# Program order in place of scheduling: the context and Fourier stage of a hybrid mixer block, and the ends of its output rows

## The chip, the cores and the metric

The kernel runs on one core of a Trainium2 chip. The metric is the device time of one launch in microseconds, lower is better. The core has TensorE (PE in the profile, with its weight loads as PEld), VectorE (DVE), ScalarE (ACT), GpSimd (POOL) and SyncE (SP, whose queue issues most DMAs). Each works through its own queue in order; semaphores tie the queues together.

## The reference

One layer of a diffusion backbone on 1024 latent tokens of 1024 channels, and 256 context tokens that are only read. A normalised input is projected once; three branches (neighbourhood attention, Fourier mixing, a convolution module) are gated, projected, merged and projected out.

```python
h  = rms_norm(x, g_pre) * (1 + scale) + shift
hc = rms_norm(ctx, g_pre) * (1 + scale_c) + shift_c
kc, vc = split(hc @ w_in[:, 512:1536])
q, k, v, g_a, u_f, g_f, c_a, c_b, g_c, s_a, s_f, s_c = split(h @ w_in)
attn = neighbourhood_attention(q, k, v, kc, vc, rpb)    # 8 x 16 window, and all context keys
f = real(fftn(u_f in 4 groups of 64, axes=(position, channel), norm="ortho"))
u = c_a * sigmoid(c_b)
u = depthwise_conv(u, w_dw, width=31) + b_dw            # 256 channels
u = silu(layer_norm(u, ln_g, ln_b)) @ w_pw              # channel norm, pointwise map
y_a, y_f, y_c = (attn * silu(g_a)) @ p_attn, ((f @ w_four) * silu(g_f)) @ p_four, (u * silu(g_c)) @ p_conv
merged = sigmoid(s_a) * y_a + sigmoid(s_f) * y_f + sigmoid(s_c) * y_c
return x + gate * rms_norm(merged @ w_out, g_post)
```

## The kernel before

Everything is float32. A product of two float32 matrices is done as three matmuls on a high and a low part of each operand (`mm3`, L141 to L143): high with high, and each high with the other's low. To split an operand, ScalarE casts it to the high part (`whi`, `hi`) and POOL or DVE subtracts (`wlo`, `lo`), both at L93. Weights come from HBM as `raw`, are split and then used; few are held, so the split of a weight waits until an earlier one is no longer read.

The stages follow each other: normalised input and the convolution's input projection (to 72 us), the context and Fourier stage with values, keys of the context and the convolution's taps (to about 226), the channel norm and the pointwise map woven into the attention's first key and query products (to 275), attention (to 480), gates, products of weight blocks in pairs, the branch projections (to 845) and the output product.

In the context and Fourier stage TensorE's work is a generator, `main_b`, whose steps are 6 or 12 matmuls; `adv(n)` takes n steps. After each step it adds `tap["rate"]` to a counter and calls `taps` for each whole one. A tap is one DVE instruction of the depthwise convolution (L476): an accumulator gets the shifted input `u` times a column. `cacc` holds the two channel blocks' results, `cb_` the odd taps. The fold (`e`, `o`, L721) turns the Fourier input into even and odd parts, which are split; `wch`, `wcl` are products of small transform matrices, split again; `eo` are the products with the long transform matrices, which arrive as weights.

TensorE alone is in program order there (`manual_schedule(engines={PE})`). For the other four the scheduler of the framework chooses the order, within program order for the chain of taps and with the first tap held behind the scaling of the context tokens (`after(..., ctx_scaled[-1])`). The channel norm comes after the stage, in pools and PSUM banks of its own: pairs of channel blocks are added and split, a matmul with ones gives `mean`, squares give `pv_`, POOL raises it to -0.5 (`rs`), a diagonal `dg` and a matmul spread it (`rsb`), and DVE and ScalarE make the swish input `zz`, 512 tokens (a half, h = 0 or 1) and one channel block at a time.

In the tail all five engines follow program order. `project(d)` makes the d-th block of 128 merged channels; `mg` is that block, and each half of it is a sum of three gated products, two additions per half (L1636). `side(d, h)` puts other work between. The output product is done in four blocks n = NP to NP + 3, each for two rows of 128 tokens, as seven products p1 to p7 of combined operands (`c0`, `c1`, ..., from `a11`, `a12` and sums `w`) with weights `wo`; `x`, `y` and `z` are PSUM banks, and `s1`, `u2`, `u3`, `s5` are copies of a bank taken between products (L1301, L1303). g2, g3, g7 add copies into quarter results; `flush` runs the end of finished quarters: square, scale, add to the rows `xt` that `x_load` fetched, store.

Of the kernel before, what the change touches and what calls it, by code (L numbers as in the profile page):

```python
# [11 lines left out]
F32 = mybir.dt.float32  # L12
# [40 lines left out]
def block_kernel(ctx: ExitStack, tc: tile.TileContext, x, ctxt, wmodp, wgate,  # L53
# [391 lines left out]
    u = [cv.tile([P, UW], F32, name=f"u{c}") for c in range(2)]  # L445
# [24 lines left out]
    cb_ = cv.tile([P, 512], F32, name="cb_")  # L470

    def fir(acc, src, ws, n, first=None):
        for k, w in enumerate(ws):
            v = src[:, k:k + n]
            if k > 0:
                tc.keep_in_program_order(dve.scalar_tensor_tensor(  # L476
                    out=acc, in0=v, scalar=w, in1=acc, op0=ALU.mult, op1=ALU.add))
            elif first is None:
                after(dve.tensor_scalar(out=acc, in0=v, scalar1=w, scalar2=None, op0=ALU.mult), ctx_scaled[-1])
# [21 lines left out]
    ca1 = [cv.tile([P, 512], F32, name=f"ca1{h}") for h in range(2)]  # L501
# [17 lines left out]
    man.enter_context(tc.manual_schedule(engines={mybir.EngineType.PE}))  # L519
    fx = ExitStack()  # L520
# [159 lines left out]

    cxs = ExitStack()
# [3 lines left out]
    ctx_scaled = [f() for f in [norm_scale(t, cx, cz, "junk") for t in cts]]  # L685
    adv(12)
# [29 lines left out]
    def fold(c):  # L716
# [8 lines left out]
        eh, el = bp.tile([P, 512], F32R, name=f"eh{c}"), bp.tile([P, 512], F32R, name=f"el{c}")  # L725
        oh, ol = bp.tile([P, 512], F32R, name=f"oh{c}"), bp.tile([P, 512], F32R, name=f"ol{c}")
# [31 lines left out]

    ae = []
# [13 lines left out]
    edge = []  # L773
    for m in range(2):
# [99 lines left out]
    psw = pools(lx, name="psw", bufs=2, space=PSUM)  # L874
    psc = pools(lx, name="psc", bufs=1, space=PSUM)
    main = main_l()
    tap["rate"] = 0.0
    adv(6)
    pwh, pwl = half_load(w_pw.rearrange("(k p) c -> p k c", p=P), [P, 2, 256], "pw", bp, b2, "lnq")
    omat = bp.tile([P, P], F32R, name="omat")  # L880
    act.activation(omat, ones, AF.Copy, scale=1.0 / 256.0)
    yc = [bp.tile([P, T], F32, name=f"yc{m}") for m in range(2)]
    vs8 = bp.tile([P, 8], F32, name="vs8")
    halves = [slice(h * 514, h * 514 + 512) for h in range(2)]

    def split_ln(src):
        hi = b2.tile([P, 512], F32R, tag="lnh", name="hi", bufs=4)
        lo = b2.tile([P, 512], F32R, tag="lnl", name="lo", bufs=4)
        split(src, hi, lo, dve)
        return hi, lo  # L890

    def pair_sum(v0, v1):
        t = b2.tile([P, 512], F32, tag="lnt", name="t")
        dve.tensor_tensor(out=t, in0=v0, in1=v1, op=ALU.add)
        return split_ln(t)

    cs = [pair_sum(cacc[0][:, s], cacc[1][:, s]) for s in halves]
    sqs = []
    for h, s in enumerate(halves):
        adv((1, 1)[h])  # L900
        mean = psw.tile([P, 512], F32, tag="sw", name="mean")
        for i in range(2):
# [988 lines left out]
```

## Time and profile before

| | |
|---|---|
| median of 3 runs | 942.32 us (941.96 to 943.43) |
| the profiled execution's own time | 943.67 us |
| its span | 941.9 us |
| TensorE busy | 890.4 us, 95% |
| VectorE busy | 725.9 us, 77% |
| ScalarE and GpSimd busy | 413.8 and 341.9 us |
| DMA | 135.85 MB |
| TensorE's granted clock, mean | 0.985 |

The span goes from the first to the last instruction; the rest of an execution's time lies around it. A row of a timeline has the start, the duration, the engine, the line and operation, the output and inputs by the program's names, the shape, and in brackets how long the engine had been idle and what it waited for. A row of a stretch has its limits, its length, then the busy time of each engine, the granted clock of TensorE, the busy share of DMA and the GB/s moved.

### The profile page before, as it was taken

What the parts mean: (1) busy time and instruction counts of PE and PEld (TensorE: products, weight loads), DVE (VectorE), ACT (ScalarE), POOL (GpSimd) and SP (SyncE); (2) the same over time, 40 slices, a digit from 0 to 9 for tenths busy, and PEclk for the clock granted to TensorE, in tenths of its full rate; (3) what the DMA queues carried; (4) which work ended last, traced back from release to release, by engine and by line L of the source; (5) the groups of instructions that cost most, each with busy time, mean ns of one, the idle gap of its engine ahead of it and who ended that gap; (6) DMA issues with size and microseconds to landing.
All of it is one profiled execution on the core that took longest, in us unless ns stands there. A gap on an engine that the chain in (4) does not pass through costs nothing. (4 is left out here: it accounts for less than half of the span.)

```text
span 941.9 us, 13235 instructions
## 1 busy us (share of the span) xinstructions
PE 890.4 (95%) x4652; PEld 746.4 (79%) x4652; DVE 725.9 (77%) x1183; ACT 413.8 (44%) x830; POOL 341.9 (36%) x310
## 2 busy tenths in 40 slices
PE   4899989999899999999999989999999999998896
PEld 2578889988678888888888877788878888775685
DVE  4656897596768999999959786557864679997985
ACT  4344523233456766776643444333343521225441
POOL 2123822164234434444420003335652048570232
PEclk9999989999999999999999999999999999999999
DMA  9703024345434444544323236423313799851323
GB/s 366 277 13 122 23 78 147 112 140 181 119 104 146 135 145 128 162 128 134 124 79 114 72 130 230 126 80 109 112 58 88 245 349 328 288 204 40 109 90 134
DMA packets 114162, 135.85 MB, mean 144 GB/s; under 512 B 5680, under 2 KB 83760, under 8 KB 114096
## 3 DMA queue, kind: packets, MB, share of 16 engines
q1 hardware_dynamic: 113952, 134.43, 43.5%
q0 software_dynamic: 144, 0.59, 0.3%
q8 instruction: 36, 0.59, 0.3%
q14 instruction: 30, 0.25, 0.1%
HBM read 102.03 MB, written 29.36 MB: 139 GB/s over the span
## 5 line engine op out<-in xcount | busy, mean ns | idle before, releaser
L141 PE MATMUL ps<-hh,whi 128*128 128x512 f32 x304 | 126.7, 417 | 0.9 <-DVE qd L851 0.9
L93 POOL TENSOR_TENSOR wlo<-raw,whi 128x512 fp32r<-128x512 f32 (+2 forms) x52 | 79.1, 1539 | 119.5 <-ACT whi L93 107.3
L143 PE MATMUL ps<-hh,wlo 128*128 128x512 f32 x304 | 119.6, 394 | 0.0
L142 PE MATMUL ps<-hl,whi 128*128 128x512 f32 x304 | 119.6, 393 | 0.0
L93 DVE TENSOR_TENSOR c<-w,c 128x512 fp32r<-128x512 f32 x64 | 53.0, 865 | 30.0 <-ACT c L93 29.9
L93 ACT CAST whi<-raw 128x512 fp32r<-128x512 f32 (+2 forms) x65 | 43.8, 705 | 69.7 <-PE ps L142 27.9
L1636 POOL TENSOR_TENSOR mg<-mg,th 128x512 f32<-128x512 f32 x30 | 50.6, 1687 | 62.3 <-DVE th L1633 60.7
L1013 POOL TENSOR_TENSOR bias<-mk,braw 128x288 f32<-128x288 bf16 (+1 forms) x64 | 54.2, 848 | 38.8 <-DVE mn L1045 37.6
L143 PEld LDWEIGHTS ps<-hh,wlo 128*128 128x128 f32 x304 | 57.5, 189 | 12.7
L141 PEld LDWEIGHTS ps<-hh,whi 128*128 128x128 f32 x304 | 57.7, 190 | 11.1 <-PE ps L143 1.3
L142 PEld LDWEIGHTS ps<-hl,whi 128*128 128x128 f32 x304 | 57.8, 190 | 9.7 <-issue 0.5
L1078 ACT CAST pt<-tp 96x384 fp32r<-96x384 f32 (+1 forms) x96 | 46.1, 514 | 43.0 <-PE tp L1071 42.3
L1084 DVE TENSOR_TENSOR pt<-tp,pt 96x384 fp32r<-96x384 f32 (+1 forms) x96 | 54.4, 593 | 2.9 <-ACT pt L1078 1.4
L1045 DVE CUSTOM_DVE_ANT_0 pr<-scb,bias 128x544 f32<-128x544 f32 (+1 forms) x64 | 49.4, 772 | 8.5 <-PE scb L1038 7.7
L1266 POOL TENSOR_TENSOR w<-raw 128x512 f32<-128x512 f32 x9 | 13.8, 1538 | 109.6 <-DMA raw<-in_w_in_dram 99.6
L1052 ACT ACTIVATE pr<-pr,mn 128x544 f32<-128x544 f32 (+1 forms) x64 | 50.8, 794 | 3.7 <-DVE mn L1045 3.6
L143 PE MATMUL ps<-gh,wlo 128*128 128x512 f32 x128 | 50.0, 390 | 0.7 <-DVE wlo L93 0.7
L141 PE MATMUL ps<-gh,whi 128*128 128x512 f32 x128 | 50.3, 393 | 0.0
L142 PE MATMUL ps<-gl,whi 128*128 128x512 f32 x128 | 50.0, 390 | 0.2 <-DVE gl L93 0.2
L1071 PE MATMUL tp<-ident,pr 128*128 128x128 f32 (+1 forms) x320 | 45.8, 274 | 1.4 <-DVE rc L1058 1.0
L93 ACT CAST c<-w 128x512 fp32r<-128x512 f32 x64 | 37.1, 617 | 22.7 <-DVE w L1266 19.5
L141 PE MATMUL x<-t,c 128*128 128x512 f32 x96 | 39.1, 407 | 6.5 <-ACT s L1301 3.3
(498 smaller groups left out, 2639.3 us busy)
## 6 DMA issues: line engine op xcount, KB each, us to landing
raw<-in_w_in_dram SPq DMA_DIRECT2D x51, 512.0 KB
wt<-in_wmodp_dram SPq DMA_DIRECT2D x16, 512.0 KB
thd<-th SPq DMA_DIRECT2D x32, 256.0 KB
th<-thd SPq DMA_DIRECT2D x32, 256.0 KB
braw<-in_rpbp_dram SPq DMA_DIRECT2D x32, 192.0 KB
vt<-vd SPq DMA_DIRECT2D x48, 128.0 KB
vd<-vs SPq DMA_DIRECT2D x20, 256.0 KB
vt<-vd SPq DMA_DIRECT2D x48, 96.0 KB
```

The source lines that it names most:

```text
L93: return act.copy(hi, src), (lo_eng or pool).tensor_tensor(out=lo, in0=src, in1=f32(hi), op=ALU.subtract)
L141: pe.matmul(ps, wh, mh, start=start, stop=False, **kw)
L142: pe.matmul(ps, wh, ml, start=False, stop=False, **kw)
L143: pe.matmul(ps, wl, mh, start=False, stop=stop, **kw)
L1013: pool.tensor_tensor(out=dst, in0=mk[:, a * 3 + MJ[j], 0:n].rearrange("p (r w) -> p r w", w=W), in1=raws[h_, min(j, 1)][:, :, 0:W], op=ALU ...
L1045: dve.tensor_tensor_reduce(out=pr, in0=sc, in1=biases[h_][:, FULL[h_](n)], scale=1.0, scalar=BIG, op0=ALU.add, op1=ALU.min, accum_out=mn)
L1052: act.activation(pr, pr, AF.Exp, scale=-1.0, bias=mn, accum_out=sums)
L1071: pe.transpose(tp[0:(kw if b < 3 else P), b], src, ident)
L1078: act.copy(pt[0:q, b0:b1, 0], tp[0:q, b0:b1])
L1084: dve.tensor_tensor(out=pt[0:q, b0:b1, 1], in0=tp[0:q, b0:b1], in1=f32(pt[0:q, b0:b1, 0]), op=ALU.subtract)
L1266: (pool if 2 < n < NP else dve).tensor_tensor(out=t, in0=i0, in1=i1, op=op)
L1636: eng.tensor_tensor(out=mg[d][:, s], in0=mg[d][:, s], in1=t, op=ALU.add)
```

## The change

Two parts, in two places of the program.

In the context and Fourier stage a second manual schedule, `bman`, covers all five engines from the stage's start to the end of the channel norm, so each engine's queue is in program order. The holds on the taps are gone. Taps are dealt by `tap["rate"]`, which is set at eight places, with taps by hand before and after the context's scaling; after the last, one step of TensorE's work goes with each tap until the taps are used up. The channel norm and the pointwise map become a generator, `channel_norm`, that says after each piece how many steps of TensorE's work come next, and it runs inside the stage, on tiles of the stage that are free by then (`oh`, `eh`, `el`, `ol`, `ca1`, `u`) and on the stage's ring of PSUM banks. The attention's first products then follow alone.

In the tail the split of `a12` for the first output block is done in `side(7, 0)`, whole, in place of two pieces after the last projection; the additions of block 7 are on DVE for both halves, where POOL had those of half 0; and in the last three output blocks p2, p6 and g2 come first, then `flush` and `x_load`, with the other flushes moved as shown.

```diff
 def fir(acc, src, ws, n, first=None):
...
-                tc.keep_in_program_order(dve.scalar_tensor_tensor(
-                    out=acc, in0=v, scalar=w, in1=acc, op0=ALU.mult, op1=ALU.add))
+                dve.scalar_tensor_tensor(out=acc, in0=v, scalar=w, in1=acc, op0=ALU.mult, op1=ALU.add)
...
-                after(dve.tensor_scalar(out=acc, in0=v, scalar1=w, scalar2=None, op0=ALU.mult), ctx_scaled[-1])
+                dve.tensor_scalar(out=acc, in0=v, scalar1=w, scalar2=None, op0=ALU.mult)
...
+    bman = ExitStack()
+    bman.enter_context(tc.manual_schedule(engines={
+        mybir.EngineType.PE, mybir.EngineType.Activation, mybir.EngineType.DVE, mybir.EngineType.Pool,
+        mybir.EngineType.SP}))
...
+    def channel_norm():
...
+        for h, s in enumerate(halves):
+            cs.append(pair_sum(h, cacc[0][:, s], cacc[1][:, s]))
+            yield 1
+        yield 2
+        for h, s in enumerate(halves):
+            mean = pm.tile([P, 512], F32, tag="m", name="mean")
+            for i in range(2):
+                pe.matmul(mean, omat, cs[h][i], start=i == 0, stop=i == 1)
+            tq = []
+            for c in range(2):
+                dve.tensor_tensor(out=cacc[c][:, s], in0=cacc[c][:, s], in1=mean, op=ALU.subtract)
+                tq.append(ln_tile("ol", c))
+                act.activation(tq[c], cacc[c][:, s], AF.Square)
+            sqs.append(pair_sum(h, *tq))
+            yield 2
+        yield 1
...
-    ctx_scaled = [f() for f in [norm_scale(t, cx, cz, "junk") for t in cts]]
-    adv(12)
+    taps(8)
+    tap["rate"] = 0.0
+    adv(2)
+    scaled = [norm_scale(t, cx, cz, "junk") for t in cts]
+    taps(1)
+    for f in scaled:
+        f()
+    tap["rate"] = 1.5
+    adv(10)
+    tap["rate"] = 1.2
...
-    for _ in main:
-        tap["acc"] += 1.6
-        while tap["acc"] >= 1.0:
-            tap["acc"] -= 1.0
-            taps(1)
-    taps(4 * CONV_K)
+    tap["rate"] = 0.6
+    while next(conv, 0) != 0:
+        adv(1)
+    tap["rate"] = 0.0
+    ln["pw"] = half_load(w_pw.rearrange("(k p) c -> p k c", p=P), [P, 2, 256], "wf", bp, b2)
+    for n in channel_norm():
+        adv(n)
+    adv(100)
+    bman.close()
...
-                    eng = dve if d == 7 and h == 1 else pool
+                    eng = dve if d == 7 else pool
...
             put(NP, "a11", mgt[0][:, :, 0:P], c0, 0)
-            ops["c0"] = c0
+            put(NP, "a12", mgt[1][:, :, 0:P], c0, 1)
             wsum(NP, 2)
...
-    a12 = mgt[1][:, :, 0:P]
-    dst = [v[:, 4:8] for v in ops["c0"]]
-    for ks in (slice(0, 3), slice(3, 4)):
-        split(a12[:, ks], *(v[:, ks] for v in dst), dve)
-    ops[n, "a12"] = dst
...
     for n in range(NP + 1, NP + 4):
         more = n + 1 < NP + 4
+        go(n, "p2", "p6", "g2")
+        flush()
         x_load(n)
-        go(n, "p2", "g2")
-        go(n, "p6")
         if more:
             prep_a(n + 1)
             wsum(n + 1, 0)
             wsum(n + 1, 1)
-        flush()
         go(n, "p5")
         go(n, "p7")
+        flush()
...
-        flush()
+        else:
+            flush()
```

How the change moves instructions is shown at three places. The first is DVE's queue at the start of the taps. Here `u` is the convolution's input after its gate, `ms` and `x` are the scaling of the context tokens (L288, L292), and a tap writes `cacc` or `cb_`. Before:

```order
L457 SCALAR_TENSOR_TENSOR u_692<-th,c_0_274 128x2x256
L457 SCALAR_TENSOR_TENSOR u_692<-th,c_1_386 128x2x256
L288 TENSOR_SCALAR ms<-ss 128x1
L292 TENSOR_SCALAR x_768<-x_768,rs 128x1024
L288 TENSOR_SCALAR ms<-ss 128x1
L292 TENSOR_SCALAR x_770<-x_770,rs 128x1024
L479 TENSOR_SCALAR cacc_694<-u_692,colt 128x513
L479 TENSOR_SCALAR cb__708<-u_692,colt 128x512
L476 SCALAR_TENSOR_TENSOR cacc_694<-u_692,colt,cacc_694 128x513
L476 SCALAR_TENSOR_TENSOR cb__708<-u_692,colt,cb__708 128x512
L476 SCALAR_TENSOR_TENSOR cacc_694<-u_692,colt,cacc_694 128x513
L476 SCALAR_TENSOR_TENSOR cb__708<-u_692,colt,cb__708 128x512
```

And with the change:

```order
L457 SCALAR_TENSOR_TENSOR u_692<-th,c_0_274 128x2x256
L457 SCALAR_TENSOR_TENSOR u_692<-th,c_1_386 128x2x256
L478 TENSOR_SCALAR cacc_694<-u_692,colt 128x513
L476 SCALAR_TENSOR_TENSOR cacc_694<-u_692,colt,cacc_694 128x513 x7
L288 TENSOR_SCALAR ms<-ss 128x1 x2
L476 SCALAR_TENSOR_TENSOR cacc_694<-u_692,colt,cacc_694 128x513
L292 TENSOR_SCALAR x_770<-x_770,rs 128x1024
L292 TENSOR_SCALAR x_772<-x_772,rs 128x1024
L476 SCALAR_TENSOR_TENSOR cacc_694<-u_692,colt,cacc_694 128x513 x7
L478 TENSOR_SCALAR cb__708<-u_692,colt 128x512
L476 SCALAR_TENSOR_TENSOR cb__708<-u_692,colt,cb__708 128x512 x11
L93 TENSOR_TENSOR wlo_969<-raw_876,whi_968 128x512
```

The taps have moved ahead of the context's scaling, and they go along one accumulator at a time, where they alternated between two.

The second place is ScalarE's queue around the norm's squares, which the weights of the third Fourier part (the `whi` with two halves) now share. Before, the norm came later in the program, and here stood the branch gates `th` and the weights:

```order
L642 ACTIVATE th<-ps 128x512
L93 CAST whi_2166<-raw_2095 128x512
L642 ACTIVATE th<-ps 128x512
L93 CAST whi_2166<-raw_2095 128x512
L93 CAST whi_2212<-raw_2172 128x512 x2
L93 CAST whi_2245<-raw_2218 128x512 x2
```

With the change (`eh` is the high part of a sum or of a sum of squares, `ol` a square, `th` a gate):

```order
L93 CAST eh<-oh 128x512 x2
L645 ACTIVATE th<-ps 128x512
L715 ACTIVATE ol<-cacc_694 128x512
L715 ACTIVATE ol<-cacc_695 128x512
L93 CAST eh<-oh 128x512
L645 ACTIVATE th<-ps 128x512
L715 ACTIVATE ol<-cacc_694 128x512
L715 ACTIVATE ol<-cacc_695 128x512
L93 CAST eh<-oh 128x512
L93 CAST whi_2223<-raw_2112 128x512 x2
L632 ACTIVATE es<-eo,ed_1712 128x128
L633 ACTIVATE es<-eo,ed_1712 128x128
```

The weights' cast stands behind the splits and squares of both halves of the norm.

The third place is DVE's queue in the second output block, around the copy `u` of bank `x` after p6 (the COPY row). `xt` rows are the end of the block before, `c` rows are splits of operands. Before:

```order
L93 TENSOR_TENSOR c_8615<-w_8581,c_8614 128x512
L93 TENSOR_TENSOR c_8615<-w_8589,c_8614 128x512
L1712 TENSOR_SCALAR v<-ssum 128x1
L1715 SCALAR_TENSOR_TENSOR v<-ssum,v 128x1
L1719 TENSOR_TENSOR y<-x,ggb 128x512
L1738 SCALAR_TENSOR_TENSOR xt<-u_8548,rs,xt 128x512
L1738 SCALAR_TENSOR_TENSOR xt<-y,rs,xt 128x512
L93 TENSOR_TENSOR c_8651<-mg_5657,c_8651 128x512
L1329 TENSOR_TENSOR s_8633<-s_8633,y 128x512
L1303 COPY u_8684<-x 128x512
L93 TENSOR_TENSOR c_8687<-mg_5656,c_8686 128x512
```

And with the change:

```order
L93 TENSOR_TENSOR c_8600<-w_8566,c_8599 128x512
L93 TENSOR_TENSOR c_8600<-w_8574,c_8599 128x512
L93 TENSOR_TENSOR c_8620<-mg_5644,c_8620 128x512
L1317 COPY u_8648<-x 128x512
L1343 TENSOR_TENSOR s_8618<-s_8618,y 128x512
L1726 TENSOR_SCALAR v<-ssum 128x1
L1729 SCALAR_TENSOR_TENSOR v<-ssum,v 128x1
L1733 TENSOR_TENSOR y<-x,ggb 128x512
L1752 SCALAR_TENSOR_TENSOR xt<-u_8533,rs,xt 128x512
L1752 SCALAR_TENSOR_TENSOR xt<-y,rs,xt 128x512
L1726 TENSOR_SCALAR v<-ssum 128x1
```

The copy has moved ahead of the older row's end, which follows it now.

More of the change, by code (lines that the diff above doesn't have):

```diff
@@ L444, in block_kernel @@
     UE, UW = 529, 1060
-    u = [cv.tile([P, UW], F32, name=f"u{c}") for c in range(2)]
+    u = [cv.tile([P, UW], F32, tag=f"u{c}", name=f"u{c}") for c in range(2)]
     cacc = [cva.tile([P, T + 2], F32, name=f"cacc{c}") for c in range(2)]
@@ L500, in block_kernel @@
         glu(0, h, c_ps[0][h], c_ps[2][h])
-    ca1 = [cv.tile([P, 512], F32, name=f"ca1{h}") for h in range(2)]
+    ca1 = [cv.tile([P, 512], F32, tag=f"ca1{h}", name=f"ca1{h}") for h in range(2)]
     for h in range(2):
@@ L747, in block_kernel @@
     adv(6)
+    tap["rate"] = 0.9
     wch = [[None, None], [None, None]]
@@ L757, in block_kernel @@
             adv(2)
+    tap["rate"] = 1.1
     ae = []
@@ L773, in block_kernel @@
     edge = []
+    tap["rate"] = 1.5
     for m in range(2):
@@ L783, in block_kernel @@
         adv(2)
-    for _ in main:
-        tap["acc"] += 1.6
-        while tap["acc"] >= 1.0:
-            tap["acc"] -= 1.0
-            taps(1)
-    taps(4 * CONV_K)
+    tap["rate"] = 0.6
+    while next(conv, 0) != 0:
[6 more added lines that the diff above has]
+    bman.close()
     fs_.close()
@@ L872, in main_l @@
         yield from k_tile(1)
[L874 to L902, printed above, removed]
-            pe.matmul(mean, omat, cs[h][i], start=i == 0, stop=i == 1)
-        tq = []
-        for c in range(2):
-            dve.tensor_tensor(out=cacc[c][:, s], in0=cacc[c][:, s], in1=mean, op=ALU.subtract)
-            tq.append(b2.tile([P, 512], F32, tag="lnq", name="t"))
-            act.activation(tq[c], cacc[c][:, s], AF.Square)
-        sqs.append(pair_sum(*tq))
@@ L926, in block_kernel @@
-    rsb = []
-    for h in range(2):
-        adv((2, 1)[h])
-        rsb.append(psw.tile([P, 512], F32, tag="sw", name="rsb"))
-        pe.matmul(rsb[h], ones, dgs[h], start=True, stop=True)
-    zz = []
-    for h, s in enumerate(halves):
-        zz.append([])
-        for c in range(2):
-            z = cacc[c][:, s]
-            dve.tensor_tensor(out=z, in0=z, in1=rsb[h], op=ALU.mult)
-            th = b2.tile([P, 512], F32, tag="lnt", name="th")
-            act.activation(th, z, AF.Tanh, scale=hb[:, c:c + 1], bias=hb[:, 2 + c:3 + c])
-            dve.tensor_scalar(out=z, in0=z, scalar1=colt[:, COL_LG + c:COL_LG + c + 1],
-                              scalar2=colt[:, COL_LB + c:COL_LB + c + 1], op0=ALU.mult, op1=ALU.add)
-            dve.scalar_tensor_tensor(out=z, in0=th, scalar=1.0, in1=z, op0=ALU.add, op1=ALU.mult)
-            zz[h].append(split_ln(z))
```

102 lines of the change are left out of this document (65 added, 37 removed).

## The prediction

> **What bounds the kernel now.** I read the page first, then the busy time by stretches, then TensorE's rows at each gap inside the two places that the change touches, and last the other engines' rows that end those gaps.
>
> ```profile
> span 941.9 us, 13235 instructions
> PE 890.4 (95%) x4652; PEld 746.4 (79%) x4652; DVE 725.9 (77%) x1183; ACT 413.8 (44%) x830; POOL 341.9 (36%) x310
> ```
>
> TensorE is busy for 890.4 of 941.9 us. The change neither adds nor removes a matmul, so it can only win idle time of TensorE or time at a low clock. The stretches show where such time lies (columns: length, busy time with instruction count of PE, PEld, DVE, ACT and POOL, then granted clock, DMA share, GB/s):
>
> ```profile
> core 0: us, PE busy (x) PEld busy (x) DVE busy (x) ACT busy (x) POOL busy (x), PEclk, DMA share, GB/s
> 73.90:118.00 44.10, 44.10 (x248) 38.16 (x247) 34.89 (x38) 19.84 (x40) 27.13 (x25) 1.00 0.19 64
> 118.00:128.00 10.00, 6.33 (x35) 6.13 (x34) 10.00 (x17) 0.38 (x1) 0.00 (x0) 0.71 0.19 54
> 156.00:200.00 44.00, 43.29 (x343) 42.26 (x342) 30.24 (x44) 13.29 (x35) 15.30 (x11) 1.00 0.42 135
> 203.27:220.69 17.42, 17.42 (x100) 15.35 (x99) 16.89 (x15) 3.91 (x7) 9.29 (x6) 1.00 0.40 122
> 235.00:250.00 15.00, 12.07 (x54) 9.69 (x52) 10.60 (x17) 6.89 (x12) 4.36 (x3) 0.89 0.57 158
> 846.00:853.00 7.00, 4.59 (x14) 3.36 (x13) 6.25 (x11) 3.14 (x5) 0.00 (x0) 0.76 0.39 147
> 883.00:890.00 7.00, 4.85 (x15) 3.51 (x14) 6.26 (x10) 2.43 (x5) 1.45 (x1) 0.77 0.67 224
> ```
>
> Four stretches have TensorE idle and a granted clock below 1: 118, 235, 846 and 883 us. In the others it is full. At 118 us DVE is busy all the time, so DVE's queue is late there, yet from 156 to 200 us DVE is idle for 14 of 44 us: its work is badly spread, not too much. The gaps themselves (start, duration, and in brackets the idle time before, with what ended it):
>
> ```profile
> 122.88 0.58 PE L141 MATMUL ps<-h_wf,h_bs 128*128 128x256 f32 x1 [3.67 <-DVE wcl L93]
> 193.35 0.39 PE L142 MATMUL eo<-wlo,ah 128*128 128x256 f32 x1 [0.71 <-POOL wlo L93]
> 243.23 0.27 PE L918 MATMUL pv__2536<-omat,hi 128*128 128x2 f32 x1 [2.41 <-ACT hi L93]
> 244.02 0.27 PE L918 MATMUL pv__2536<-omat,lo 128*128 128x2 f32 x1 [0.52 <-DVE lo L93]
> 266.73 0.47 PE L141 MATMUL ps<-hh,whi 128*128 128x512 f32 x1 [0.90 <-DVE qd L851]
> 849.25 0.80 PE L143 MATMUL y<-wo,c0o 128*128 128x512 f32 x1 [2.41 <-DVE c0o L93]
> 849.84 0.63 PE L141 MATMUL y<-wo,c0o 128*128 128x512 f32 x1
> 870.01 0.50 PE L142 MATMUL x<-wo,c 128*128 128x512 f32 x1 [0.70 <-DVE wo L93]
> 885.67 0.50 PE L141 MATMUL x<-wo,c 128*128 128x512 f32 x1 [2.15 <-DVE u L1303]
> ```
>
> After each gap of 2.15 us or more the clock falls; after gaps of 0.90 or less it does not. What the low clock costs follows from the stretches: (1 - 0.71) x 10 = 2.9 us after the gap of 3.67, (1 - 0.89) x 15 = 1.65 after 2.41, (1 - 0.76) x 7 = 1.7 and (1 - 0.77) x 7 = 1.6 in the tail. So a gap of some 2.3 us really costs about 4 us.
>
> [...]
>
> **The change part by part: the taps.** They are the depthwise convolution's steps on DVE, now started at once and dealt out at a rate for each step. The rows that price them:
>
> ```profile
> 72.66 1.27 DVE L457 SCALAR_TENSOR_TENSOR u<-th,c 128x512 f32<-128x512 f32 x2
> 81.23 0.48 DVE L479 TENSOR_SCALAR cacc<-u,colt 128x513 f32<-128x513 f32 x1
> 137.72 1.54 DVE L476 SCALAR_TENSOR_TENSOR cacc<-u,wsum,cacc 128x512 f32<-128x512 f32 x2
> 203.27 17.39 DVE L476 SCALAR_TENSOR_TENSOR cacc<-u,wsum,cacc 128x512 f32<-128x512 f32 x15
> 158.71 0.37 ACT L93 CAST bh<-ps 128x256 fp32r<-128x256 f32 x1 [1.59 <-PE ps L143]
> ```
>
> The operand u is done at 73.9 and the first tap runs at 81.23, so 7.3 us of DVE are given to it. Taps on one accumulator follow each other after 1.54 - 0.75 = 0.79 us. Fifteen of them took 17.39 us where 11.8 were due; POOL was busy for 9.29 us of that stretch, so each us of POOL stretches DVE by 0.6. Up to the first wcl I count, in DVE's new queue, 32 taps (25 us), four combining steps (2.8), two context scalings (1.4), a weight split (0.6), the folds (2.4), the two u (1.3) and small ones (1): 34.5 us. POOL's work before it, less what lies in waits, adds 0.6 x 20 = 12. That makes 73.9 + 46.5 = 120.4, and wcl's end about 121. The gap at 119 us falls from 3.67 to about 2.3: **+1.4 us**, and its low clock from 2.9 to the 1.65 that the gap of 2.41 costs: **+1.25**. Bounds: 0 if wcl comes no earlier, 6.6 if gap and low clock go altogether.
>
> In program order POOL's split of the weights that the Fourier products wait for at 193.35 stands behind ScalarE's value copies, which wait for DVE, whose value steps now stand between taps. The 0.71 us there can rise; I take **-0.8**, bounds 0 and -2 (the nearest gap of a split that waits in a queue, 2.41).
>
> The last tap must be done before the mean's matmuls, which come after 203.9 in the old count of matmuls. DVE is tied to TensorE by the last bl, whose cast was ready at 158.71 and now at 156.1. After it I count 34 taps (26.8) and 8.7 of value, key and combining steps: 35.5; POOL's 15.30 of the old stretch at 0.6 add 9.2. So the taps end at 201 to 202, sum and split take 2 more, and TensorE comes at 203.9 - 2.65 + 0.8 = 202: a wait of 0 to 3 us. I take **-1.0**; the long bound is a rival below.
>
> **The channel norm inside the stage.** It removes the waits for norm pieces at 243.23, 244.02 and the one for qd at 266.73, and the low clock after them: 2.41 + 0.52 + 0.90 + 1.65 = **+5.5 us** (+4.6 if qd still waits). What it puts in is seen from the grouped rows of the old norm, 227 to 262 us (the last columns: busy us, mean ns, idle before):
>
> ```profile
> L906 DVE TENSOR_TENSOR cacc<-cacc,mean 128x512 f32<-128x512 f32 x4 | 2.5, 682 | 0.0
> L894 DVE TENSOR_TENSOR t<-t 128x512 f32<-128x512 f32 x2 | 3.1, 1564 | 0.4 <-ACT t L908 0.4
> L93 DVE TENSOR_TENSOR lo<-t,hi 128x512 fp32r<-128x512 f32 x4 | 2.7, 690 | 0.1
> L936 DVE TENSOR_TENSOR cacc<-cacc,rsb 128x512 f32<-128x512 f32 x4 | 2.6, 681 | 0.8 <-PE rsb L930 0.8
> L908 ACT ACTIVATE t<-cacc 128x512 f32<-128x512 f32 x4 | 2.5, 628 | 1.5 <-DVE cacc L906 1.5
> L938 ACT ACTIVATE th<-cacc,hb 128x512 f32<-128x512 f32 x4 | 3.3, 817 | 3.9 <-DVE cacc L936 3.2 <-PE rsb L930 0.7
> L93 ACT CAST hi<-t 128x512 fp32r<-128x512 f32 x4 | 2.5, 620 | 6.6 <-DVE t L894 6.6
> L93 ACT CAST whi<-raw 128x512 fp32r<-128x512 f32 x2 | 1.2, 616 | 0.0
> L93 POOL TENSOR_TENSOR wlo<-raw,whi 128x512 fp32r<-128x512 f32 x2 | 3.0, 1501 | 8.6 <-ACT whi L93 8.6
> ```
>
> ScalarE's queue now has the weights of the third Fourier part behind the norm's squares and splits of both halves. From the first mean's start, T: matmuls 0.45, two subtractions 1.36, a square 0.63, a sum 0.7 (a tap-like DVE step with POOL quiet), a split on ScalarE 0.62 and DVE 0.69 bring the first half to T + 4.5; the second half's two subtractions, square, sum and split bring ScalarE to T + 8.1, whi to T + 8.7, and POOL's wlo (at its shorter time of about 1.3) to T + 10.1. Between, TensorE has 12 + 2 wide matmuls at 0.227 and 24 half-wide ones at 0.117, so it arrives at T + 6.3. It waits 3.8, say **-4.0**, in two pieces of about 2.4 and 1.3, and the first is long enough for one spell of low clock, **-1.65**. The last pieces, each a product with rsb, a tanh, two more DVE steps and a split, some 3.9 us in series, can make the second half's pointwise map late by 0.5 to 1.7: **-1.0**. Bounds of this part: -3 if weights slip ahead, -10 if a low clock follows every piece.
>
> **The tail.** In these rows lie the two gaps of the output rows:
>
> ```profile
> 837.15 6.64 POOL L1636 TENSOR_TENSOR mg<-mg,th 128x512 f32<-128x512 f32 x4
> 841.26 1.40 DVE L93 TENSOR_TENSOR c0o<-mg,c0o 128x512 fp32r<-128x512 f32 x1
> 846.71 0.69 DVE L1636 TENSOR_TENSOR mg<-mg,th 128x512 f32<-128x512 f32 x1
> 848.64 0.75 DVE L93 TENSOR_TENSOR c0o<-mg,c0o 128x384 fp32r<-128x384 f32 x2
> 884.93 0.69 DVE L1303 COPY u<-x 128x512 f32<-128x512 f32 x1
> ```
>
> The last half-block's sums end on POOL at 843.8, and the split that they release runs on DVE only at 848.64, behind the other half's five steps. Now DVE does both sums (two steps, 0.6 apart) by 842.5 and both splits by 844, and TensorE wants the second at 846.5: the 2.41 and their 1.7 of low clock go. But the two sums and the longer split push the other half's steps back by about 0.6, and the next operand, the sum of blocks cast by ScalarE and split by DVE, comes at 850.0 where TensorE now comes at 848.9, and its low part costs 0.2 more: a new wait of 1.3, too short for a low clock by the rows above. Net **+2.8**, bounds 1.0 and 4.1. At 883 the copy u ran at 884.93 behind six steps of an older row's end; it now stands in front of them, and can run as soon as its matmuls are through, 2.4 us before TensorE needs it: 2.15 + 1.6 = **+3.75**, bounds 2 and 3.75. Behind it the row ends (five DVE steps of about 0.7) and the load of x wait instead; they have the next product's 2.7 us of matmuls and the one after, and the x rows are needed a whole block of products later. Between the two, the wo splits (0.70 at 870.01 and two like it) are paced by DVE and ScalarE, and can take back some: **-0.5**, bound -2. The page's rows after 934 us, the last row's end, keep their order.
>
> **The sum.** 1.4 + 1.25 - 0.8 - 1.0 + 5.5 - 4.0 - 1.65 - 1.0 + 2.8 + 3.75 - 0.5 = 5.75 us. The profiled execution took 943.67 (its span and 1.8 around it), 1.35 above the median of 942.32; I take the sum from the median: 936.6 us. Of it the stage has -0.3, its own new waits eating what it wins, and the tail 6.05. Attention and what follows keep their order and start about when they did.
>
> **The rivals.** *The stage becomes clean.* If no low clock follows in the stage and the weights' wait stays under 2 us, the first gap goes (+6.6 for 2.65) and the norm costs -3 for -6.65: 936.6 - 3.95 - 3.65 = 929. For it speaks that DVE has 14 us to spare from 156 to 200; against it, that ScalarE's queue holds the weights behind the norm. *The tail moves its waits.* If the wo splits pace the tail, c0o gives 1.0 and u 2, and 2 are lost: 5 less, 941.6. For it: three gaps on these splits lie between; against: ScalarE itself waits for TensorE's z before them. *DVE becomes the bound at the mean (slower).* If POOL holds DVE for its whole time, the 15.30 us count fully, not at 0.6: the taps end 6.1 later, the mean's wait is 7.1, with the 2.9 of low clock that 3.67 brought: 9.0 worse, 945.6. It decides as soon as DVE's chain slips by more than the 5.75 gained. Against it: the 15 taps above, 5.6 late for 9.29.
>
> [...]
>
> **How the numbers follow.** What this kernel's measurement can tell from no change is 0.2%, 1.9 us. Forecast (931.5 to 940): 0.54; clean stage (926 to 931.5): 0.16; moved tail (940 to 942.5): 0.14; DVE late (above 942.5): 0.14; below 926: 0.02. Faster than 940.4 are the first two, the last and a third of the moved tail's: 0.77. Within 0.2% lie most of the moved tail and a little of the late DVE: 0.11. Slower: 0.12. The range leaves out the lower part of the clean stage and most of the late DVE: 928 to 943; the forecast's own is 931.5 to 940.
>
> **What would show it.** Right: the first tap at about 74 us; the gap before ps<-h_wf,h_bs near 2.3; mean's matmuls at 201 to 204 with a wait under 3; a gap on whi or wlo of 2 to 5 us just after; none on c0o, a short one on z<-wo,c behind it; none on u. Wrong: a wait for el or a tap above 5 us before the mean, a granted clock below 1 in the tail, or the stage as a whole, up to attention's first scores, more than 4 us longer or shorter than before.

## The result, and the profile after

The changed kernel takes 956.82 us (955.80 to 961.23, 4 runs) where the kernel before took 942.88 (941.96 to 944.37, 4 runs): a ratio of 1.0137, 95% interval 1.0106 to 1.0167. The ratios here and below are the record's estimates and need not be the quotients of the medians (1.0148 here). By the medians it is slower by 13.9 us; 936.6 was forecast, with a range of 928 to 943. The page of the profiled execution begins (span, then busy time by engine):

```profile
span 954.5 us, 13233 instructions
PE 893.5 (94%) x4652; PEld 749.5 (79%) x4652; DVE 721.4 (76%) x1184; ACT 413.4 (43%) x829; POOL 336.6 (35%) x308
```

TensorE's busy time is 3.1 us longer, which is matmuls at a low clock (mean granted clock 0.981, before 0.985); no other engine has more work. The number of matmuls is the same, so the two traces can be laid side by side by the number of the matmul, counted from 0. The table gives how much later than before matmul n starts:

| matmul | before, us | after, us | later by |
|---|---|---|---|
| 600 (behind the gap at 119) | 129.74 | 128.12 | -1.6 |
| 900 | 166.08 | 171.05 | +5.0 |
| 1100 (the second value pass) | 190.08 | 195.05 | +5.0 |
| 1172 (the mean's first in the changed order) | 203.68 | 218.84 | +15.2 |
| 1500 (just behind the attention's first scores) | 275.59 | 296.23 | +20.6 |
| 4300 (before the output product) | 839.88 | 858.40 | +18.5 |
| 4651 (the last) | 933.46 | 946.14 | +12.7 |

The stage costs 20.6 us instead of the forecast 0.3, and the tail wins 5.8 instead of 6.05. Where it happens, the busy time by stretches shows (columns as before: length, busy time and count of PE, PEld, DVE, ACT and POOL, granted clock, DMA share, GB/s):

```profile
118.00:128.00 10.00, 6.72 (x45) 6.51 (x43) 8.57 (x11) 0.54 (x2) 2.82 (x2) 0.83 0.19 54
150.00:162.00 12.00, 8.12 (x48) 7.72 (x48) 9.87 (x18) 4.40 (x10) 1.76 (x2) 0.77 0.65 213
162.00:196.00 34.00, 34.00 (x281) 34.00 (x281) 28.05 (x37) 6.11 (x17) 5.58 (x3) 0.98 0.20 64
196.00:212.00 16.00, 8.37 (x36) 7.29 (x35) 14.29 (x20) 4.99 (x11) 7.03 (x5) 0.68 0.49 164
212.00:225.00 13.00, 13.00 (x69) 11.17 (x69) 9.86 (x12) 5.19 (x10) 3.94 (x3) 1.00 0.26 90
225.00:235.00 10.00, 6.62 (x32) 6.18 (x31) 3.33 (x9) 4.67 (x11) 6.01 (x5) 0.66 0.46 135
235.00:262.00 27.00, 26.00 (x113) 21.01 (x113) 14.03 (x25) 9.82 (x17) 3.85 (x4) 0.87 0.11 35
866.00:872.00 6.00, 4.46 (x19) 3.07 (x18) 5.18 (x8) 3.09 (x4) 0.00 (x0) 1.00 0.21 79
898.00:905.00 7.00, 7.00 (x33) 5.70 (x31) 6.78 (x13) 3.09 (x7) 2.48 (x3) 1.00 0.36 116
```

Before, TensorE was full from 156 to 200 and from 203 to 220 us. Now it is idle for a third to a half of the time around 153, 200 and 228 us, each time with a low clock behind. The tail's two stretches now have a clock of 1.00. TensorE's rows at the gaps (in brackets the idle time before the row and what ended it):

```profile
122.54 0.58 PE L141 MATMUL ps<-h_wf,h_bs 128*128 128x256 f32 x1 [3.28 <-DVE wcl L93]
155.91 0.39 PE L141 MATMUL ps<-whi,hh 128*128 128x256 f32 x1 [2.92 <-ACT whi L93]
157.26 0.58 PE L142 MATMUL ps<-wlo,hh 128*128 128x256 f32 x1 [0.96 <-POOL wlo L93]
203.09 0.58 PE L141 MATMUL eo<-whi,ah 128*128 128x256 f32 x1 [6.45 <-ACT whi L93]
204.81 0.58 PE L142 MATMUL eo<-wlo,ah 128*128 128x256 f32 x1 [1.14 <-POOL wlo L93]
227.95 0.42 PE L141 MATMUL eo<-whi,ah 128*128 128x256 f32 x1 [2.45 <-ACT whi L93]
229.29 0.58 PE L142 MATMUL eo<-wlo,ah 128*128 128x256 f32 x1 [0.93 <-POOL wlo L93]
259.61 0.51 PE L141 MATMUL ps<-zz,h_wf 128*128 128x512 f32 x1 [0.78 <-ACT zz L93]
869.17 0.50 PE L141 MATMUL z<-wo,c 128*128 128x512 f32 x1 [1.54 <-ACT c L93]
```

Three times TensorE waits for `whi`, the cast of the next weights on ScalarE, though ScalarE is busy for less than half of the time. ScalarE's queue ahead of the worst of them, and DVE's in the same time:

```profile
195.28 0.65 ACT L604 CAST vs<-ps 128x256 fp32r<-128x256 f32 x2 [2.74 <-DVE vs L605]
198.72 0.65 ACT L604 CAST vs<-ps 128x256 fp32r<-128x256 f32 x2 [2.79 <-DVE vs L605]
202.15 0.37 ACT L604 CAST vs<-ps 128x256 fp32r<-128x256 f32 x1 [2.79 <-DVE vs L605]
202.42 1.14 ACT L93 CAST whi<-raw 128x512 fp32r<-128x512 f32 x2
```

```profile
196.03 2.32 DVE L476 SCALAR_TENSOR_TENSOR cacc<-u,wsum,cacc 128x512 f32<-128x512 f32 x3
198.27 0.42 DVE L605 TENSOR_TENSOR vs<-ps,vs 128x256 fp32r<-128x256 f32 x1
199.12 0.42 DVE L605 TENSOR_TENSOR vs<-ps,vs 128x256 fp32r<-128x256 f32 x1 [0.44 <-ACT vs L604]
199.47 2.32 DVE L476 SCALAR_TENSOR_TENSOR cacc<-u,wsum,cacc 128x512 f32<-128x512 f32 x3
201.70 0.42 DVE L605 TENSOR_TENSOR vs<-ps,vs 128x256 fp32r<-128x256 f32 x1
215.11 0.68 DVE L693 TENSOR_TENSOR oh<-cacc,cacc 128x512 f32<-128x512 f32 x1
```

The second cast of each pair of value tiles waits for DVE's subtraction of the first (a row with x2 joins it to the first cast of the next pair). DVE in its turn does three taps between two pairs, and is itself held up 0.44 us in every pair until ScalarE has done the second cast. The two engines go through the value tiles hand over hand at 3.4 us a pair, DVE all but without a pause, and the weights' cast stands behind the last pair. DVE's last row, at 215.11, is the sum for the first mean, which follows the last tap.

### The profile page after: what moved, and what is told of

It is laid out like the page before. It is cut to its first block, busy times and chain, and to the rows that moved or that the text cites. A ratio compares the mean times of both kernels' runs of the same rounds, so it can differ in the third digit from the quotient of the medians.

```text
span 954.5 us, 13233 instructions
## 1 busy us (share of the span) xinstructions
PE 893.5 (94%) x4652; PEld 749.5 (79%) x4652; DVE 721.4 (76%) x1184; ACT 413.4 (43%) x829; POOL 336.6 (35%) x308
## 5 line engine op out<-in xcount | busy, mean ns | idle before, releaser
L93 POOL TENSOR_TENSOR wlo<-raw,whi 128x512 fp32r<-128x512 f32 (+2 forms) x52 | 74.9, 1460 | 145.6 <-ACT whi L93 145.5
L93 DVE TENSOR_TENSOR c<-w,c 128x512 fp32r<-128x512 f32 x64 | 50.8, 832 | 30.0 <-ACT c L93 29.9
L1650 POOL TENSOR_TENSOR mg<-mg,th 128x512 f32<-128x512 f32 x28 | 47.7, 1704 | 62.1 <-DVE th L1647 60.7
L143 PEld LDWEIGHTS ps<-hh,wlo 128*128 128x128 f32 x304 | 57.6, 190 | 12.7
L141 PEld LDWEIGHTS ps<-hh,whi 128*128 128x128 f32 x304 | 57.9, 191 | 10.5 <-ACT yc L758 0.6
L93 DVE TENSOR_TENSOR c<-raw,c 128x512 fp32r<-128x512 f32 x36 | 35.8, 1034 | 12.9 <-ACT c L93 12.6
```

What stands on the lines that cost most here:

```text
L93: return act.copy(hi, src), (lo_eng or pool).tensor_tensor(out=lo, in0=src, in1=f32(hi), op=ALU.subtract)
L141: pe.matmul(ps, wh, mh, start=start, stop=False, **kw)
L143: pe.matmul(ps, wl, mh, start=False, stop=stop, **kw)
L1650: eng.tensor_tensor(out=mg[d][:, s], in0=mg[d][:, s], in1=t, op=ALU.add)
```

## The experiments

The kernel before was timed again beside each set of experiments: 943.91, 943.86, 943.83 and 944.13 us. The ratios are to these. One limit for reading single traces first: where the stage's code is that of before (the next run), its 1500th matmul came 3.6 us later than in the first trace of it, so a difference of less than about 4 us at one matmul is read here only where the rows show its cause.

**The two parts apart.** The kernel before with the tail of the change (the diff from L1632 on), and the change with the old tail.

> The kernel before with the tail's part of the change alone (the sums of block 7 on DVE, a12 split early, p6 ahead of the older row's end). Theory: the two parts add up, so the tail alone wins what the trace of the change shows there, 5.8 us: about 937.1 where before is 942.9, with no gap on c0o and none on u at p7. Rival: the tail's gain is owed to the stage's new timing (buffers and loads that come at other times); then it wins 2 us or less.

> The change without its tail. Theory: the stage alone costs what the trace shows up to attention's first scores, 20 to 21 us: about 962 to 963. Rival (the parts hang together): under 958.

The tail alone: 940.66 us (937.51 to 942.39), ratio 0.9958 (0.9936 to 0.9980), 4.0 us faster by the ratio (3.3 by the medians), between the theory's 5.8 and the rival's 2. The stage alone: 963.03, ratio 1.0184 (1.0130 to 1.0238), as expected. The parts add up within the noise, so the search is in the stage. In the tail, TensorE gains 5.8 us from the 4300th matmul to the end, and the new wait for the sum of blocks is there, 1.54 us where 1.3 was forecast:

```profile
852.45 0.50 PE L141 MATMUL z<-wo,c 128*128 128x512 f32 x1 [1.54 <-ACT c L93]
```

**Whose order.** The change with TensorE's order alone fixed:

```diff
-    bman.enter_context(tc.manual_schedule(engines={
-        mybir.EngineType.PE, mybir.EngineType.Activation, mybir.EngineType.DVE, mybir.EngineType.Pool,
-        mybir.EngineType.SP}))
+    bman.enter_context(tc.manual_schedule(engines={mybir.EngineType.PE}))
```

> The change with program order in the stage for TensorE alone; the other four engines are ordered by the scheduler again, the norm stays inside the stage and the taps are dealt as in the change. Theory (the loss is program order: value steps behind taps on DVE hold ScalarE's queue, in which the weights' casts stand): the gaps on whi at 152.7 and 196.4 us go, 15 us or more of the stage's 20 come back, 937 to 943. Rival (the norm inside the stage, or the tiles that it shares, cost it): the time stays above 950.

946.48 us, ratio 1.0024 (0.9992 to 1.0057): 10 us come back; the time lies between the 937 to 943 of the theory and the 950 of its rival. The waits for whi are gone, and others are there, since nothing holds the taps back any more (39 have started by 119 us, 27 before), the two longest:

```profile
112.61 0.39 PE L142 MATMUL ps<-wlo,hh 128*128 128x256 f32 x1 [3.96 <-DVE wlo L93]
133.56 0.58 PE L141 MATMUL ps<-h_wf,h_bs 128*128 128x256 f32 x1 [7.82 <-DVE wcl L93]
```

The 1100th matmul is 15.4 us late, the 1500th 9.1: with the scheduler's order the norm inside the stage wins 6.4 us of what the early taps cost. The place of the norm is therefore not bad in itself.

**No taps among the value tiles.** The change, with the taps that fall due while value tiles are finished kept back and dealt two at a time behind them:

```diff
     def taps(n):
-        for _ in range(n):
-            next(conv, None)
+        owed[0] += n
+        if owed[1]:
+            return
+        for _ in range(min(owed[0], 2 * n)):
...
+            owed[1] = wi == 1 and t < 9
```

> The change, with program order on all five engines, but no taps are dealt while value tiles are being finished; they follow afterwards, two at a time. Theory: value subtractions no longer stand behind taps, ScalarE gets through its copies, and the weights come: the gaps on whi at 152.7 (3.1, with 1.2 on wlo and low clock, 6.6 in all) and 196.4 (6.6 and 1.6, 10.2 in all) shrink to under 1.5 each, so the part up to the mean wins 10 to 15 us, of which a later end of the taps takes back up to 8: 942 to 950. Rival (the weights are late for their raw load or their buffer): both gaps stay, 955 or more.

961.58 us, ratio 1.0169: the theory's 942 to 950 missed. The waits at 152 and 196 go, as it said, and the same taps are late elsewhere: some 6 us for a wlo on DVE at 174, and at the mean

```profile
223.79 0.79 PE L718 MATMUL mean<-eh,omat 128*128 128x512 f32 x1 [7.32 <-ACT eh L93]
```

So the pairs of value casts were only one place where it showed. The theory that ScalarE's place in the order is the whole cause fell here.

**The old dealing of taps with the norm inside.** TensorE's order alone fixed, taps kept in place and held behind the context scaling as before, at the old rates, and once at 1.2 a step throughout.

```diff
-                dve.scalar_tensor_tensor(out=acc, in0=v, scalar=w, in1=acc, op0=ALU.mult, op1=ALU.add)
+                tc.keep_in_program_order(dve.scalar_tensor_tensor(
+                    out=acc, in0=v, scalar=w, in1=acc, op0=ALU.mult, op1=ALU.add))
...
+                after(dve.tensor_scalar(out=acc, in0=v, scalar1=w, scalar2=None, op0=ALU.mult), ctx_scaled[-1])
...
-    tap["rate"] = 0.6
+    tap["rate"] = 1.6
     while next(conv, 0) != 0:
```

> The change with TensorE's order alone fixed, and the taps dealt and held as before it (first tap behind the context scalings, each tap kept in place, the old rates); norm and pointwise map inside the stage, tail as changed. Theory: the stage is as before up to the 1100th matmul (190 us), the norm inside it wins the 6.4 us that it won with TensorE's order alone fixed, the tail 4.0 to 5.8: total 931 to 934. Rival (taps end at 220 as before, so that the norm has no matmuls left to hide behind): a wait of 5 to 10 us at the mean or the pointwise map, 938 to 944.

> As the one with the taps dealt as before, but at a rate of 1.2 for every step from the start, so that the taps end some 10 us earlier and lie thicker where DVE had idle time (156 to 200 us). Theory: 929 to 934, with no wait at the mean over 2 us. Rival (taps crowd the folds and wcl ahead of 130 us): the gap at 119 to 123 us grows by 3 or more and the total is 936 to 942.

958.66 us (951.78 to 960.15; the trace is of an execution at the lower end) and 950.37, ratios 1.0146 and 1.0069. Both theories missed; both rivals were right in kind, but the totals that they gave (up to 944) missed too. At the old rates the first mean waits 0.64 and 1.92 us for the taps and the second 5.74, at 1.2 a step the gap before 126 us grows to 5.8 and the mean still waits:

```profile
126.12 0.58 PE L141 MATMUL ps<-h_wf,h_bs 128*128 128x256 f32 x1 [5.78 <-DVE wcl L93]
215.34 0.80 PE L709 MATMUL mean<-eh,omat 128*128 128x512 f32 x1 [5.44 <-ACT eh L93]
```

In each of these runs DVE is late, ahead of 150 us or at the mean or at both. In the kernel before the taps ended still later, at 220.7, but the first mean came at 235.63: the change puts it 174 matmuls earlier, and DVE's slack is gone.

**The other queues out of the way, one after the other.** First both casts of a pair ahead of both subtractions, and the weights' cast ahead of the last pair:

```diff
+            if wi == 1 and t == 9:
+                emit_split(i_v[ch][wi] + 2)
...
                     act.copy(vs[:, :, 0:4:3], psv)
+                    pair.append((vs, psv))
+                for i, (vs, psv) in enumerate(pair):
                     dve.tensor_tensor(out=vs[:, :, 1:3], in0=psv, in1=f32(vs[:, :, 0:4:3]), op=ALU.subtract)
```

> The change with two edits that take ScalarE's queue out of the way: the two casts of a pair of value tiles run one behind the other ahead of DVE's two subtractions, and the cast and split of the weights for the Fourier part stand ahead of the last pair of value casts. Theory A (DVE's queue is the bound of the stage, and the gaps on whi at 152.7 and 196.4 are only where it first shows): both gaps fall under 2.5 us, but TensorE then comes to the mean some 8 to 15 us earlier than DVE's taps end, which follow TensorE by no more than the first gap's 6.6; a new wait at the mean of 5 to 10 us, total 948 to 953. Theory B (ScalarE's queue alone): both gaps go and nothing takes their place, 6.6 + 10.2 = 16.8 less, total 939 to 942.

955.95 us, ratio 1.0140 (1.0091 to 1.0190), neither 948 to 953 nor 939 to 942. The wait at 153 is gone (the 1100th matmul comes 1.4 us earlier than before, not 5.0 later). At 194 the wait is there again, for the next weights, and not at the mean. The queues that hold them now, SP's and ScalarE's:

```profile
182.00 15.00 SPq L611 DMA_DIRECT2D vd<-vs  x10
197.09 0.41 SPq L108 DMA_DIRECT2D raw<-in_w_in_dram  x1
```

```profile
198.44 0.38 ACT L548 ACTIVATE kctx<-ps 64x256 fp32r<-64x256 f32 x1 [5.57 <-DVE kctx L551]
202.48 1.14 ACT L93 CAST whi<-raw 128x512 fp32r<-128x512 f32 x2 [3.66 <-DMA raw<-in_w_in_dram]
```

SP issues the load of the weights behind ten stores of value tiles, and the stores wait for DVE's subtractions; the changed kernel has the same order (ten stores over 15.65 us from 187.67, the load at 203.42). So next SP's order was left to the scheduler, which moves the loads ahead of the stores; and, by itself, the weights of the third Fourier part were cast ahead of the norm's second squares; and then all of these together, with the pointwise weights loaded ahead of the last taps:

```diff
-        mybir.EngineType.PE, mybir.EngineType.Activation, mybir.EngineType.DVE, mybir.EngineType.Pool,
-        mybir.EngineType.SP}))
+        mybir.EngineType.PE, mybir.EngineType.Activation, mybir.EngineType.DVE, mybir.EngineType.Pool}))
...
+            if h == 1:
+                emit_split(i_dft[1][0])
             tq = []
```

> The change with the value casts in pairs and the weights' cast ahead of the last pair, and SP's order left to the scheduler: the loads of the next weights and of the pointwise weights then stand ahead of the ten value stores, which wait for DVE's subtractions. Theory C (in program order every queue of the stage is late through DVE: the 8.4 us that whi was late at 194.5 in the run without this edit is SP's queue, loads behind value stores): that gap goes to under 1.5 us; DVE's taps then end last, at 204 to 206, and the mean is waited for, 2 to 5 us; total 947 to 951. Rival (the load was late for another reason, such as its buffer): the gap at 194.5 stays over 5 us and the total over 953.

> The change with one line moved: the cast and split of the third Fourier part's weights are issued ahead of the second half's squares of the norm, not behind them. Theory (the 2.45 and 0.93 us waited for them at 225 and 229 and the low clock behind are the norm's cost in the stage): the two gaps fall to under 1 us together and with them some low clock, 3 to 5 us less, total 952 to 954. Rival (the norm's second half is then as late as the weights were): a new wait at the variance's matmuls of 1 us or more and a total over 955.

> All of these: value casts in pairs, weights' cast ahead of the last pair, SP's order by the scheduler, pointwise weights loaded and split ahead of the last taps, and the third Fourier part's weights ahead of the norm's second squares. Theory C: as without the last two, less 3 to 6 us for the norm: 942 to 947, and what stays over the kernel before is the wait at the mean for DVE's taps. Rival (what is moved forward pushes other steps back as it did each time so far): 948 to 953.

With SP free: 953.58 us, ratio 1.0101 (1.0068 to 1.0134). The gap at 194 falls from 8.4 to 4.8 us, nearer to the rival's 5 than to the theory's 1.5, and the total is above the theory's 951 and just in the rival's range (over 953). With the norm's weights ahead: 954.61, ratio 1.0111 (1.0063 to 1.0159), an interval that holds the changed kernel's own ratio; in the trace the waits of 2.45 and 0.93 shrink to 0.95 and 0.27, the clock stays at 1.00 there, and a wait of 1.83 for `zz` with a spell of 3.4 us at a clock of 0.50 comes in at 255, so that 3.3 us of the stage's 20.6 go, where 3 to 5 were expected; the total is 0.6 above the expected 954. All together: 948.64, ratio 1.0052 (1.0028 to 1.0076), where theory C said 942 to 947 and its rival 948 to 953: in its total the rival is right. From the mean's matmul to the 1494th the stage then needs 71.8 us, against 76.2 with the change and 71.0 for as many matmuls before. What is left lies ahead of the mean:

```profile
200.63 0.79 PE L141 MATMUL ps<-hh,whi 128*128 128x512 f32 x1 [4.78 <-ACT whi L93]
```

```profile
199.55 0.38 ACT L547 ACTIVATE kctx<-ps 64x256 fp32r<-64x256 f32 x1 [5.11 <-DVE kctx L550]
199.96 2.18 ACT L93 CAST whi<-raw 128x512 fp32r<-128x512 f32 x4
```

```profile
160.00:190.00 30.00, 29.56 (x247) 29.36 (x246) 28.71 (x39) 6.77 (x19) 6.07 (x4) 1.00 0.27 88
190.00:203.00 13.00, 6.63 (x40) 5.21 (x39) 12.24 (x17) 4.76 (x11) 5.30 (x4) 0.80 0.46 163
```

```profile
200.42 8.29 DVE L476 SCALAR_TENSOR_TENSOR cacc<-u,wsum,cacc 128x512 f32<-128x512 f32 x6
208.63 0.68 DVE L697 TENSOR_TENSOR oh<-cacc,cacc 128x512 f32<-128x512 f32 x1
```

The load of these weights is now issued at 180.53 and their cast names no DMA any more; it stands behind the cast of a key tile that waits for DVE. DVE (the third busy column) is at work for 40.95 of 43 us from 160 to 203 (29.43 in the kernel before), and ends the taps at 208.6. Each edit took one queue out from behind DVE, and the next queue that is tied to it then showed the lateness.

**DVE's own work.** If that is so, less work on DVE must do what no order did. In the change, and in the run with all the edits, 24 of the 32 taps of the last filter pass are left out, in place, with the order of all else kept: 12 for each of the two channel blocks, which lie at 114 to 141 us and at 193 to 214 us in the changed kernel.

```diff
             v = src[:, k:k + n]
+            if first is not None and k % 4 > 0:
+                yield
+                continue
```

> The change with 12 of the 16 taps left out in each channel's last filter pass (24 taps, 19 us of DVE; the output is not the reference's); the order of all else, TensorE's included, is kept. Theory A (DVE's queue too long from 178 us on): the value subtractions run without taps between them, the gap on whi at 196.4 falls from 6.45 to under 2, the mean is not waited for, total 943 to 947 (about 10 less; the first gap at 152.7, which lies ahead of these taps, stays). Theory B (the queue's order, not its length): gaps stay, total above 953.

> The run with all five edits to ScalarE's, SP's and the norm's order, and beside them 24 of the last filter pass's 32 taps left out (19 us of DVE, so the output is not the reference's; the order of all else is kept). Theory C (with the other queues out of the way DVE's own work, busy 41 of 43 us from 160 to 203, is what holds TensorE at 195 and at the mean): no gap over 1.2 us from 180 to 215, the mean's first matmul at 203 to 206 in place of 212.9, total 7 to 10 less than with the taps, 938 to 942. Rival (the last key cast and the loads stay late whatever DVE has to do): a gap of 3 us or more at 190 to 200, total 944 or more.

The change without these taps: 948.18 us, ratio 1.0046 (1.0021 to 1.0071), 8.6 less than with them where about 10 were expected, and above the expected 943 to 947. The gap before the first Fourier product (3.28 us at 119) goes too, with the taps left out near it, and the one at 196 falls to 3.82 and 1.14 in two pieces, not under 2. There the hand over hand with ScalarE is left, and a value cast that waits 1.91 us for the store of an earlier value tile. With the edits as well: 938.16, ratio 0.9946 (0.9923 to 0.9969), 10.5 less than with the taps.

```profile
190.00:203.00 13.00, 10.54 (x49) 8.35 (x48) 8.22 (x10) 4.61 (x9) 6.73 (x4) 1.00 0.52 176
192.22 0.50 PE L141 MATMUL ps<-hh,whi 128*128 128x512 f32 x1 [1.48 <-ACT whi L93]
188.84 0.37 ACT L609 CAST vs<-ps 128x256 fp32r<-128x256 f32 x1 [1.91 <-DMA vd<-vs]
```

The mean comes at 201.8, and the granted clock is 1.00 from 118 to 128 us and from 140 us to the end of the stage. The gap of 1.48 is a little over the 1.2 that was expected; behind it stands the last row, a wait for a store of a value tile, and no longer DVE, which is idle for 3.19 us then. Theory C holds: in this order DVE's work ahead of the mean is the bound, and program order passes it on through ScalarE's and SP's queues. How much the missing taps would win in the kernel before was not run; of the 11.6 us that the traces show won here up to the 1500th matmul, 4.4 come ahead of the 600th, at the first gap, and 6.7 from there to the mean.

## Why the prediction was wrong

**The step that failed** is the one that says POOL's split of the weights "stands behind ScalarE's value copies, which wait for DVE, whose value steps now stand between taps", with "-0.8, bounds 0 and -2". The mechanism is the one that came; its size was given without a source, bounded by the nearest gap of a split that waits in a queue, 2.41 us, and not worked out along DVE's queue. There it would have read: five pairs, three taps and a hand-over each, 3.4 us a pair. At 196 it cost 10.2 us, gap and low clock together (matmuls 1100 to 1172), and 6.6 more at 153, at the first value pass, which the prediction left out altogether. These 16.8 us are most of the 20.6.

**The mean, -1.0.** There is no wait in the changed kernel, where TensorE came 15 us late: the sum for the mean ran at 215.11, while matmul 1172 started at 203.68 before. The forecast of DVE's end, 201 to 202, is the same mistake from the other side. Its sum of 44.7 us for the work behind the last bl was right: with all queues free it took 46.0 (162.67 to 208.63). It was hung on ScalarE's cast for that bl, "now at 156.1"; DVE itself only got to it at 162.7 there, and at 165.1 in the changed kernel, behind taps and value steps in its own queue.

**The rivals.** "DVE becomes the bound at the mean (slower)", at 945.6 with a chance of 0.14, had the engine and the sign, and the place in some of the experiments only. Its price rested on POOL holding DVE up fully, and that isn't what came: with all edits, 39 taps and combining steps took 38.4 us, 7.6 more than at 0.79 each, with 15.1 us of POOL beside them, and it was the start that was late. That the lateness would come out through other queues first was in no rival. The other two did not come.

**The norm inside the stage.** The removed waits and the new ones were about right: 3.38 us for the weights where 4.0 was forecast, in two pieces of 2.45 and 0.93 (forecast 2.4 and 1.3), and 1.0 at the pointwise map as forecast. The low clock behind was the mis-sized term: -1.65 was taken, and the clock was at half for 13.5 us, which costs up to half of that, 6.7, since matmuls of 128x512 start every 0.43 us at half clock in this trace and every 0.23 at full; the last section has its rows. From the mean to the 1494th matmul this part cost 5.2 us (76.2 against 71.0), where the terms named here come to a loss of 1.15.

**The first gap, +1.4 and +1.25.** It fell from 3.67 to 3.28, +0.4, and its low clock from 6.75 to 3.5 us, +1.6. The sum is nearer than its parts, and it can't be put down to the change: in the trace of the tail alone, whose stage is that of before, the 600th matmul also came 1.4 us earlier, with one spell of 3.4 us behind a gap of 3.62.

**The tail, +6.05.** Right: both gaps and their low clock went, the new wait was 1.54, and the trace gives 5.8; timed alone it is 4.0 (1.9 to 6.0).

Of its own marks for being wrong, "the stage as a whole ... more than 4 us longer" is what happened. Between the 1500th and the 4000th matmul the changed kernel regains 2.2 us, and the tail's run 1.8. Nearly all of it (1.9 and 1.6) lies between the 3000th and the 3500th, where the trace of before has two spells of low clock, at 555.7 and 593.2 us, and these two have none; in the five experiments whose traces have both spells at most 0.3 us is regained there. The last section has the gap ahead of the first of these spells in both traces, of nearly the same length in each.

## What to carry over

When several engines go over to program order, follow the engine with the least slack through its queue, step by step, from the last point where it is known to be on time, and only then cost the waits of the others: in these runs each instruction on another queue that waited for it carried its lateness to all that stood behind, loads on SP's queue included (the load at 203.42 us, behind ten stores over 15.65). A gap in one queue is then worth what the next one behind it leaves over, as four edits in a row showed; take work off the late engine instead, or leave its order to the scheduler. Of this change only the tail is worth keeping: with the old stage it runs at 940.66 us, faster than both.

## What was unexpected of the hardware

In these traces the time at half clock behind a gap did not follow the gap's length. In windows of a quarter us the granted clock was at half for 3.5 us behind the gap of 3.28 us at 119, for 6.75 behind 2.92 and 0.96 at 153, for 10.25 around 6.45 and 1.14 at 196, and for 13.5 behind 2.45 and 0.93 at 225; before, for 6.75 behind 3.67 and 3.5 behind 2.41.

By the trace's own record of the clock, the changed kernel's four spells up to the last matmul begin at 122.34, 156.47, 200.85 and 228.15 us and last 3.41, 6.83, 10.24 and 13.65: one to four times 3.413 us. They begin 10, 23 and 31 times 3.413 us behind the first; in the trace of before those at 245.07, 555.68, 593.23, 849.23 and 886.78 begin 36, 127, 138, 213 and 224 times 3.413 us behind the first, at 122.19. A piece is here a stretch of 3.413 us, counted from the first spell's start in each trace. The last spell, piece by piece, and two of TensorE's rows in it:

```profile
228.15:231.57 3.42, 2.49 (x11) 2.28 (x11) 1.41 (x4) 2.33 (x7) 3.42 (x3) 0.50 0.05 8
231.57:234.98 3.41, 3.41 (x18) 3.41 (x17) 0.29 (x2) 0.00 (x0) 2.41 (x3) 0.50 0.63 192
234.98:238.39 3.41, 3.41 (x17) 3.31 (x16) 0.91 (x5) 1.14 (x2) 0.34 (x1) 0.50 0.38 115
238.39:241.81 3.42, 3.42 (x10) 2.65 (x9) 2.70 (x4) 0.00 (x0) 3.16 (x3) 0.50 0.00 0
241.81:245.22 3.41, 3.41 (x15) 2.46 (x14) 1.08 (x4) 0.82 (x1) 0.00 (x0) 1.00 0.00 0
231.81 0.21 PE L724 MATMUL pv__2287<-omat,eh 128*128 128x2 f32 x1
236.08 0.21 PE L724 MATMUL pv__2315<-omat,eh 128*128 128x2 f32 x1
```

The first piece has the idle 0.93 us in it. The second and the third look full, but each holds eight of the norm's matmuls with two columns of output, from 231.81 and from 236.08 us on, 1.56 us of time each. The fourth has wide matmuls alone, and the clock is full behind it. In the other spells of this trace and of before's, the clock was at half again behind the pieces with 0.60, 0.69, 0.78 and 2.83 us of idle time, and full behind those with 0.20 or less. The spell at this place also lasts over 12 us in three more traces (the stage alone, the casts in pairs, SP free). No run here takes the two-column matmuls out, so whether they have to do with it was not shown.

In these two traces, from 30 us to the last matmul, the ten pieces at full clock with half clock behind them had 2.03 to 3.41 us of idle time, and those with full clock behind them 1.78 or less. No one amount divides the two: a piece with 1.47 had half clock behind it in the change without the taps, and one with 1.77 in the run with the norm's weights ahead. The same matmul of the attention, before and with the change:

```profile
554.36 0.50 PE L141 MATMUL x<-t,c 128*128 128x512 f32 x1 [2.67 <-ACT s L1301]
574.68 0.50 PE L141 MATMUL x<-t,c 128*128 128x512 f32 x1 [2.65 <-ACT s L1315]
```

Before, 2.09 us of the gap fell into one piece, and the clock was at half from 555.7 to 559.1. With the change two pieces met in the gap, at 572.90, with 0.88 and 1.78 us of idle time, and the clock stayed at 1.00. So the prediction's reading that the clock falls after each gap of 2.15 us or more holds for the gaps that it shows, and not for every gap. The same code also had spells of different length in two executions (the old norm: 3.5 us in the one, 6.75 in the other, up to 252.3 us). For the cost of a low clock the changed kernel's spells of 3.41 to 13.65 us give an estimate of 1.7 to 6.8 us, half of each.
